# Scores from row halves, the coefficient on GpSimd, and token norms on ScalarE, in a two-layer hybrid backbone

## The chip, the cores and the metric

The kernel runs on one core of one Trainium2 chip. The metric is device time of one execution in microseconds (us). Three runs of the kernel before took 2230.95, 2233.83 and 2234.59 us, median 2233.83. A fourth execution was profiled; it took 2234.37 us, its trace spans 2232.6 us, and TensorE was granted 0.978 of its full clock on the mean.

## The reference, cut to what matters

Two layers work on 640 tokens of width 1024: 512 noisy latents (four tiles of 128) and 128 context tokens (one tile). Each layer norms and modulates the tokens, projects them, runs three mixers side by side (an RWKV-7 scan, a differential attention, a long convolution), projects their outputs together, norms, gates and adds, and then does the same around a squared-ReLU MLP. The change touches the attention and the RMS norm of the tokens:

```python
def _rmsnorm(x, g):
    xf = x.astype(jnp.float32)
    y = xf * lax.rsqrt(jnp.mean(xf * xf, axis=-1, keepdims=True) + RMS_EPS)
    return (y * g.astype(jnp.float32)).astype(x.dtype)

def _diff_attention(q, k, v, lam):
    ...
    def block(qblk):
        s = jnp.einsum('bqhmd,bkhmd->bhmqk', qblk, k).astype(jnp.float32) * scale
        p = jax.nn.softmax(s, axis=-1)
        wts = p[:, :, 0] - lam * p[:, :, 1]
        return jnp.einsum('bhqk,bkhe->bqhe', wts.astype(v.dtype), v)
    ...
```

There are four heads. A head has two maps (`m`), each with queries and keys of 64 dimensions, and values of 128. A latent query sees 640 keys (512 latents and 128 of a cache), a context query sees the 128 context keys.

## The kernel before, in words

The program is a long list of instructions for five engines: TensorE (PE), VectorE (DVE), ScalarE (ACT), GpSimd (POOL) and the DMA queues. A scheduler chooses the order on each engine when the program is built; after that each engine goes through its list in order, and an instruction that waits holds up all behind it.

One layer runs in this order: input columns of the convolution and the scan, the attention's columns, operands of the scan, attention, the scan itself (with the next modulations), the output projection with norm, and the MLP with norm. In the trace the attention of the first layer lies at 378 to 470 us and that of the second at 1443 to 1537 us. A prologue (0 to about 112 us) computes filters and modulations and norms the five token tiles.

`attention` (L609) goes over 4 heads times 5 token tiles, 20 units per layer, as a pipeline of three stages: at step n `at_scores` of unit n, `at_values` of unit n-1, `at_out` of unit n-2. At the third tile of a head, `at_head` loads the next head.

`at_head` (L636) fills two tiles of `[128, 2, 640]` floats. `kr` holds the keys with both maps stacked, map 0 in rows 0 to 63 and map 1 in rows 64 to 127: 512 latent keys after rotary embedding, the cache's 128, the context's 128. `qp` holds the queries twice, padded: plane 0 has map 0's queries in its upper rows and zeros below, plane 1 the other way round. So a matmul over all 128 rows gives the scores of one map. The zeros come from two memsets on POOL (L645, L646), the context's queries from two DMAs (L649), and the last add of the rotary embedding is done in two halves of 64 rows on DVE (L659). `at_v` (L666) takes a third tile, `vt`, for the values: five tiles of 128 tokens and the cache.

`at_scores` (L670) does for each map one matmul of 512 columns (L682) and one of 128 (L683), or for the context's unit one of 128 (L685), into the PSUM pool `pss` of two buffers; a minimum along the row on DVE (`amin`, L687) and an exponential on ACT that also gives the row's sum (`pexp`, `asum`, L689). Then the two maps are put together: DVE takes the reciprocal of the second sum (`arec`, L692), makes from it the coefficient `acf` = first sum x reciprocal x minus lambda (L694), and adds the second map times `acf` to the first (L698). POOL squares the first sum (`ae`, L696). `at_values` (L701) transposes the result on PE (`pst`), copies it (`awt`) and multiplies it with the values (`pso`, L714). `at_out` (L717) takes a sum of squares on ACT (`ass`, L723), makes the output's scale in three POOL instructions (`asm` L725, `ars` L727, `aon` L728), and transposes the scaled output on PE (`psy`).

`norm_tok` (L1422) norms one tile of 128 tokens: ACT squares it with a sum (L1426), `rstd` makes the scale on POOL, and DVE multiplies the tile by it (L1428). It is called 20 times: for the five tiles in the prologue (`xl`), and 15 times on `acc`, inside the stretches where the projections end and each layer begins.

The matmuls on the scores are on plain 32-bit floats, which PE does in two passes.

Of the kernel before, what the change touches and what calls it, by code (L numbers as in the profile page):

```python
# [12 lines left out]
AF = mybir.ActivationFunctionType  # L13
ALU = mybir.AluOpType
# [3 lines left out]
P = 128  # L18
NL = 2
TL = 512  # L20
TC = 128
T = TL + TC
NT = T // P
# [88 lines left out]
class Net:  # L112
# [524 lines left out]
    def at_head(self, l, h):  # L637

        nc, I = self.nc, self.I
        rot = [(i + 16) % 32 for i in range(32)]  # L640
        kr = self.at_tile("kr").rearrange("p a t -> p (a t)")
        nc.sync.dma_start(kr[:, TL:T], I["cache_kT"][l, h])
        nc.sync.dma_start(kr[:, T:T + TC], self.Qd[4 + h][:, TL:])
        qp = self.at_tile("qp")
        nc.gpsimd.memset(qp[64:, 0], 0.0)  # L645
        nc.gpsimd.memset(qp[:64, 1], 0.0)  # L646
        for m in range(2):
            r = slice(64 * m, 64 * m + 64)
            nc.sync.dma_start(qp[r, m, TL:], self.Qd[h][r, TL:])  # L649
        for isq in range(2):  # L650
            u, sh = (self.t(self.pS, [P, T], F32, "S", nm)[:, :TL] for nm in ("ql", "rsh"))
            nc.sync.dma_start(u, self.Qd[h if isq else 4 + h][:, :TL])
            nc.vector.stream_shuffle(sh, u, rot)
            nc.gpsimd.tensor_tensor(out=sh, in0=sh, in1=self.rope[:, 1], op=ALU.mult)
            nc.vector.tensor_tensor(out=u, in0=u, in1=self.rope[:, 0], op=ALU.mult)
            if isq:
                for m in range(2):
                    r = slice(64 * m, 64 * m + 64)
                    nc.vector.tensor_tensor(out=qp[r, m, :TL], in0=u[r], in1=sh[r], op=ALU.add)  # L659
            else:  # L660
                nc.vector.tensor_tensor(out=kr[:, :TL], in0=u, in1=sh, op=ALU.add)
        return {"kr": kr, "qp": qp}

    def at_v(self, l, h, head):
        vt = self.at_tile("vt").rearrange("p a t -> p (a t)")[:, :(NT + 1) * P].rearrange("p (j t) -> p j t", t=P)
        hs = slice(h * P, (h + 1) * P)  # L666
        self.nc.sync.dma_start(vt[:, :NT], self.Vd[:, :, hs])
        self.nc.sync.dma_start(vt[:, NT], self.I["cache_v"][l][:, hs])
        head["vt"] = vt

    def at_scores(self, u, pool):

        nc, H, j = self.nc, u["head"], u["j"]
        lat = j < 4
        nk = u["nk"] = T if lat else TC
        pm = []
        s = self.t(pool, [P, 2], F32, "asum")
        for m in range(2):
            q = H["qp"][:, m, j * P:(j + 1) * P]
            ps = self.t(self.pss, [P, 1024], F32, "pss")  # L680
            if lat:
                nc.tensor.matmul(ps[:, :TL], q, H["kr"][:, :TL], start=True, stop=True)  # L682
                nc.tensor.matmul(ps[:, TL:T], q, H["kr"][:, TL:T], start=True, stop=True)  # L683
            else:
                nc.tensor.matmul(ps[:, :TC], q, H["kr"][:, T:T + TC], start=True, stop=True)  # L685
            mn = self.t(pool, [P, 1], F32, "amin")
            nc.vector.tensor_reduce(out=mn, in_=ps[:, :nk], axis=AX.X, op=ALU.min)  # L687
            pe = self.t((self.pwh, self.pwl)[m], [P, 1024], F32, ("wh", "wl")[m], "pexp")[:, :T]
            nc.scalar.activation(pe[:, :nk], ps[:, :nk], AF.Exp, bias=mn, scale=-1.0, accum_out=s[:, m:m + 1])  # L689
            pm.append(pe)  # L690
        rc = self.t(pool, [P, 1], F32, "arec")
        nc.vector.reciprocal(rc, s[:, 1:2])  # L692
        cf = self.t(pool, [P, 1], F32, "acf")
        nc.vector.scalar_tensor_tensor(out=cf, in0=s[:, 0:1], scalar=rc, in1=self.nlam, op0=ALU.mult, op1=ALU.mult)  # L694
        e0 = u["e0"] = self.t(pool, [P, 1], F32, "ae0", bufs=4)
        nc.gpsimd.tensor_tensor(out=e0, in0=s[:, 0:1], in1=s[:, 0:1], op=ALU.mult)  # L696
        w = u["w"] = pm[0]
        nc.vector.scalar_tensor_tensor(out=w[:, :nk], in0=pm[1][:, :nk], scalar=cf, in1=w[:, :nk],  # L698
                                       op0=ALU.mult, op1=ALU.add)
# [722 lines left out]
    def norm_tok(self, x, out, pool, junk=None):  # L1422
        nc = self.nc
        ss = self.t(pool, [P, 1], F32, "ss")
        kw = {} if junk is None else {"saturate": False}
        nc.scalar.activation(out if junk is None else junk, x, AF.Square, accum_out=ss, **kw)  # L1426
        r = self.rstd(pool, ss, D, 1e-6, [P, 1])
        nc.vector.tensor_scalar(out=out, in0=x, scalar1=r, scalar2=None, op0=ALU.mult)  # L1428

    def act_tiles(self):  # L1430
        x = [self.t(self.pA, [P, 2, T], F32R, "A", f"act{k}") for k in range(KD)]
# [360 lines left out]
```

## Time and profile before

| | |
|---|---|
| runs | 2230.95, 2233.83, 2234.59 us |
| profiled execution | 2234.37 us |
| its span in the trace | 2232.6 us |
| mean granted clock of TensorE | 0.978 |
| PE busy | 94% of the span |
| DVE, ACT, POOL busy | 64%, 38%, 36% |

The difference of 1.8 us between the span and the profiled execution's time lies around the trace and is kept as it is. A share of busy time is a mean over stages with different limits, so what a stage is worth has to be read from that stage. The chain of work that ended last is followed back from the last instruction; an engine's time counts in full only where it lies on it. Matmuls overlap, so the time from one matmul's start to the next one's start says more than a matmul's own duration.

### The profile page before, as it was taken

Reading aid. Unit: us, or ns where it says so; the run is one execution under the profiler, and the core shown is the slowest. Engines: PE = TensorE matmul, PEld = TensorE weight load, DVE = VectorE, ACT = ScalarE, POOL = GpSimd, SP = SyncE. Lnnn points to the kernel's source line nnn. Section 1 sums busy time; section 2 is a strip of 40 time slices with the busy share of each in tenths; the row PEclk is TensorE's granted clock in tenths of the full one; section 3 lists DMA queues with packets and bytes.
Section 4 is the critical chain, followed back from the end, with each engine's and each line's share of the span. In section 5 each row is a group of like instructions: output and inputs, shape, how many; then the busy total and the mean of one; then the engine's idle time right before and its main releaser. Section 6 shows DMA issues by size and latency. Waiting matters only on the chain.

```text
span 2232.6 us, 34700 instructions
## 1 busy us (share of the span) xinstructions
PE 2104.0 (94%) x13620; PEld 1811.5 (81%) x13620; DVE 1425.3 (64%) x2102; ACT 849.7 (38%) x1670; POOL 806.9 (36%) x775
## 2 busy tenths in 40 slices
PE   6999998889999899999999999988999989999998
PEld 3799996667788789898988999766788788989896
DVE  6667648856675845564766674886576584637475
ACT  4542344653442623131324334465344352313131
POOL 5434434631112424251522443464112342524251
PEclk8999999999999999999999999999999999999999
DMA  8244432145405122222254243223501512222233
GB/s 306 82 153 146 137 101 80 43 146 190 154 18 197 66 82 70 88 81 78 86 179 167 97 130 101 87 67 129 188 23 56 182 44 95 80 73 93 77 104 123
DMA packets 86072, 245.46 MB, mean 110 GB/s; under 512 B 12195, under 2 KB 24995, under 8 KB 85908
## 3 DMA queue, kind: packets, MB, share of 16 engines
q1 hardware_dynamic: 80148, 222.34, 29.6%
q0 software_dynamic: 5760, 20.91, 3.0%
q8 instruction: 107, 1.75, 0.3%
q14 instruction: 57, 0.47, 0.1%
HBM read 214.80 MB, written 28.87 MB: 109 GB/s over the span
## 4 chain that ended last, share of the span: by engine, by line
PE 37%; DVE 8%; issue 5%; DMA 4%; POOL 4%; ACT 2%; SPq 0%; POOLq 0%; DVEq 0%; ACTq 0%
PE psA L388 5%; PE psB L176 5%; PE psB L177 5%; PE psB L175 5%; PE psF L177 2%; PE psF L176 2%; PE psF L175 2%; DMA ffb<-in_w_ff_dram 1%; DMA wr<-in_w_mod_dram 1%; PE b L1023 1%; POOL fft L457 1%; DVE wl L143 1%; DVE ffr L497 1%; PE pss L682 1%; PE psD L175 1%
## 5 line engine op out<-in xcount | busy, mean ns | idle before, releaser
L388 PE MATMUL psA<-act,wh 128*128 128x320 f32 x1472 | 300.4, 317 | 0.9 <-ACT uhr L1513 0.5
L388 PEld LDWEIGHTS psA<-act,wh 128*128 128x128 f32 x1472 | 236.9, 191 | 9.5 <-issue 6.8
L177 PE MATMUL psB<-wh,f 128*128 128x512 f32 x560 | 218.1, 389 | 0.0
L176 PE MATMUL psB<-wl,f 128*128 128x512 f32 x560 | 218.0, 389 | 0.0
L143 POOL TENSOR_TENSOR wl<-wr,wh 128x1024 fp32r<-128x1024 f32 x42 | 103.8, 2472 | 305.1 <-ACT wh L147 150.6
L175 PE MATMUL psB<-wh,f 128*128 128x512 f32 x560 | 209.1, 389 | 0.0
L388 PE MATMUL psA<-act,wl 128*128 128x320 f32 x736 | 179.5, 316 | 2.4 <-DVE wl L143 2.4
L143 DVE TENSOR_TENSOR wl<-wr,wh 128x1024 fp32r<-128x1024 f32 x84 | 109.7, 1306 | 83.0 <-ACT wh L147 74.6
L147 ACT CAST wh<-wr 128x1024 fp32r<-128x1024 f32 x75 | 78.7, 1049 | 188.3 <-PE psB L177 87.7
L457 POOL TENSOR_TENSOR fft<-ffb 128x512 f32<-128x512 f32 x56 | 92.1, 1644 | 129.7 <-DVE wl L143 56.2
L388 PEld LDWEIGHTS psA<-act,wl 128*128 128x128 f32 x736 | 126.4, 191 | 5.2 <-DVE wl L143 3.4
L177 PEld LDWEIGHTS psB<-wh,f 128*128 128x128 f32 x560 | 105.1, 188 | 22.0
L175 PEld LDWEIGHTS psB<-wh,f 128*128 128x128 f32 x560 | 105.1, 188 | 21.6
L176 PEld LDWEIGHTS psB<-wl,f 128*128 128x128 f32 x560 | 105.1, 188 | 21.6
L147 ACT CAST f<-ffr 128x640 fp32r<-128x640 f32 x64 | 43.7, 726 | 154.2 <-DVE ffr L497 154.2
L1052 DVE TENSOR_TENSOR x<-b,cmask 128x512 f16<-128x512 f32 x120 | 80.3, 685 | 31.8 <-PE b L1051 31.3
L1061 ACT CAST t<-px 128x512 f16<-128x512 f32 x100 | 58.5, 588 | 103.8 <-PE px L1056 103.0
L149 DVE CAST wh<-wr 128x1024 fp32r<-128x1024 f32 x51 | 41.8, 819 | 84.1 <-PE psB L177 63.9
L505 DVE TENSOR_TENSOR ffr<-ffr,psF 128x320 f32<-128x320 f32 x140 | 67.3, 481 | 36.5 <-POOL ffr L505 20.3
L505 POOL TENSOR_TENSOR ffr<-ffr 128x320 f32<-128x320 f32 x56 | 54.2, 967 | 92.6 <-DVE ffr L505 87.6
L1023 PE MATMUL b<-ZR,bp 128*128 128x256 f32 x320 | 85.6, 392 | 0.8 <-ACT awt L147 0.7
L176 PE MATMUL psF<-ffS,sh 128*128 128x320 f32 x256 | 80.0, 313 | 5.8 <-DVE ffS L143 5.8
(463 smaller groups left out, 6000.9 us busy)
## 6 DMA issues: line engine op xcount, KB each, us to landing
wr<-in_w_mod_dram SPq DMA_DIRECT2D x83, 512.0 KB
wr<-in_w_ff_dram SPq DMA_DIRECT2D x72, 512.0 KB
wr<-in_w_in_dram SPq DMA_DIRECT2D x46, 512.0 KB
x<-x SPq DMA_DIRECT2D x30, 512.0 KB
ffa<-in_w_ff_dram SPq DMA_DIRECT2D x28, 512.0 KB
ffb<-in_w_ff_dram SPq DMA_DIRECT2D x28, 512.0 KB
dft<-in_k_dftf_dram POOLq DMA_DIRECT2D x16, 512.0 KB, 7.6
dft<-in_k_dfti_dram POOLq DMA_DIRECT2D x16, 512.0 KB, 5.0
```

The lines of the kernel that those rows point to most:

```text
L143: eng.tensor_tensor(out=l, in0=src, in1=h.bitcast(F32), op=ALU.subtract)
L147: self.nc.scalar.copy(out, in_)
L149: self.nc.vector.tensor_copy(out, in_)
L175: nc.tensor.matmul(out, a[0], b[0], start=first, stop=False)
L176: nc.tensor.matmul(out, a[0], b[1], start=False, stop=False)
L177: nc.tensor.matmul(out, a[1], b[0], start=False, stop=last)
L388: self.nc.tensor.matmul(ps[:, hf, :320], (h, l)[a][:, k * P:(k + 1) * P], act[b][k][:, hf * 320:hf * 320 + 320], start=k == 0 and i == 0, ...
L457: sub = lambda o, x, y: nc.gpsimd.tensor_tensor(out=o, in0=x, in1=y, op=ALU.subtract)
L505: add = lambda o, a, b, e=nc.vector, op=ALU.add: e.tensor_tensor(out=o, in0=a, in1=b, op=op)
L1023: nc.tensor.matmul(ps[:, 2 * e:2 * e + 2], bp[:, q, e], s["ZR"][:, :, j], start=True, stop=True)
L1052: nc.vector.tensor_tensor(out=vw(x16), in0=vw(ps), in1=cm(i), op=ALU.mult)
L1061: nc.scalar.copy(t16, ps1)
```

## The change

Four things change.

1. The queries are no longer padded. `at_head` writes all 128 rows of the rotated queries by one add into `vq`, and a map's scores are taken by matmuls over the 64 rows `r` of that map alone, in queries and keys. The memsets of zeros go, and the two DMAs of context queries become one, into the free columns 768 to 895 of `kr`.
2. A head has two tiles instead of three: the values take columns 0 to 767 of `vq` and the latent queries columns 768 to 1279. `vq` is taken in `at_head` and filled with values by `at_v` as before.
3. The coefficient `acf` is made by a `tensor_scalar` of two per-row scalars on POOL instead of DVE's `scalar_tensor_tensor`.
4. In `norm_tok` the multiplication by the scale is an activation `Copy` with a per-row scale on ACT instead of a DVE `tensor_scalar`.

```diff
--- before.py
+++ after.py
@@ -638,31 +638,24 @@
 
         nc, I = self.nc, self.I
         rot = [(i + 16) % 32 for i in range(32)]
+
         kr = self.at_tile("kr").rearrange("p a t -> p (a t)")
+        vq = self.at_tile("vq").rearrange("p a t -> p (a t)")
         nc.sync.dma_start(kr[:, TL:T], I["cache_kT"][l, h])
         nc.sync.dma_start(kr[:, T:T + TC], self.Qd[4 + h][:, TL:])
-        qp = self.at_tile("qp")
-        nc.gpsimd.memset(qp[64:, 0], 0.0)
-        nc.gpsimd.memset(qp[:64, 1], 0.0)
-        for m in range(2):
-            r = slice(64 * m, 64 * m + 64)
-            nc.sync.dma_start(qp[r, m, TL:], self.Qd[h][r, TL:])
+        nc.sync.dma_start(kr[:, T + TC:T + 2 * TC], self.Qd[h][:, TL:])
+        q = vq[:, 768:]
         for isq in range(2):
             u, sh = (self.t(self.pS, [P, T], F32, "S", nm)[:, :TL] for nm in ("ql", "rsh"))
             nc.sync.dma_start(u, self.Qd[h if isq else 4 + h][:, :TL])
             nc.vector.stream_shuffle(sh, u, rot)
             nc.gpsimd.tensor_tensor(out=sh, in0=sh, in1=self.rope[:, 1], op=ALU.mult)
             nc.vector.tensor_tensor(out=u, in0=u, in1=self.rope[:, 0], op=ALU.mult)
-            if isq:
-                for m in range(2):
-                    r = slice(64 * m, 64 * m + 64)
-                    nc.vector.tensor_tensor(out=qp[r, m, :TL], in0=u[r], in1=sh[r], op=ALU.add)
-            else:
-                nc.vector.tensor_tensor(out=kr[:, :TL], in0=u, in1=sh, op=ALU.add)
-        return {"kr": kr, "qp": qp}
+            nc.vector.tensor_tensor(out=q if isq else kr[:, :TL], in0=u, in1=sh, op=ALU.add)
+        return {"kr": kr, "vq": vq}
 
     def at_v(self, l, h, head):
-        vt = self.at_tile("vt").rearrange("p a t -> p (a t)")[:, :(NT + 1) * P].rearrange("p (j t) -> p j t", t=P)
+        vt = head["vq"][:, :(NT + 1) * P].rearrange("p (j t) -> p j t", t=P)
         hs = slice(h * P, (h + 1) * P)
         self.nc.sync.dma_start(vt[:, :NT], self.Vd[:, :, hs])
         self.nc.sync.dma_start(vt[:, NT], self.I["cache_v"][l][:, hs])
@@ -676,13 +669,12 @@
         pm = []
         s = self.t(pool, [P, 2], F32, "asum")
         for m in range(2):
-            q = H["qp"][:, m, j * P:(j + 1) * P]
+
+            r = slice(64 * m, 64 * m + 64)
+            q = H["vq"][r, 768 + j * P:768 + (j + 1) * P] if lat else H["kr"][r, T + TC:T + 2 * TC]
             ps = self.t(self.pss, [P, 1024], F32, "pss")
-            if lat:
-                nc.tensor.matmul(ps[:, :TL], q, H["kr"][:, :TL], start=True, stop=True)
-                nc.tensor.matmul(ps[:, TL:T], q, H["kr"][:, TL:T], start=True, stop=True)
-            else:
-                nc.tensor.matmul(ps[:, :TC], q, H["kr"][:, T:T + TC], start=True, stop=True)
+            for a, b, o in ((0, TL, 0), (TL, T, TL)) if lat else ((T, T + TC, 0),):
+                nc.tensor.matmul(ps[:, o:o + b - a], q, H["kr"][r, a:b], start=True, stop=True)
             mn = self.t(pool, [P, 1], F32, "amin")
             nc.vector.tensor_reduce(out=mn, in_=ps[:, :nk], axis=AX.X, op=ALU.min)
             pe = self.t((self.pwh, self.pwl)[m], [P, 1024], F32, ("wh", "wl")[m], "pexp")[:, :T]
@@ -691,7 +683,7 @@
         rc = self.t(pool, [P, 1], F32, "arec")
         nc.vector.reciprocal(rc, s[:, 1:2])
         cf = self.t(pool, [P, 1], F32, "acf")
-        nc.vector.scalar_tensor_tensor(out=cf, in0=s[:, 0:1], scalar=rc, in1=self.nlam, op0=ALU.mult, op1=ALU.mult)
+        nc.gpsimd.tensor_scalar(out=cf, in0=s[:, 0:1], scalar1=rc, scalar2=self.nlam, op0=ALU.mult, op1=ALU.mult)
         e0 = u["e0"] = self.t(pool, [P, 1], F32, "ae0", bufs=4)
         nc.gpsimd.tensor_tensor(out=e0, in0=s[:, 0:1], in1=s[:, 0:1], op=ALU.mult)
         w = u["w"] = pm[0]
@@ -1425,7 +1417,7 @@
         kw = {} if junk is None else {"saturate": False}
         nc.scalar.activation(out if junk is None else junk, x, AF.Square, accum_out=ss, **kw)
         r = self.rstd(pool, ss, D, 1e-6, [P, 1])
-        nc.vector.tensor_scalar(out=out, in0=x, scalar1=r, scalar2=None, op0=ALU.mult)
+        nc.scalar.activation(out, x, AF.Copy, scale=r)
 
     def act_tiles(self):
         x = [self.t(self.pA, [P, 2, T], F32R, "A", f"act{k}") for k in range(KD)]
```

The lines behind `at_head` move up by 8 in the changed kernel (L682 is L677, L694 is L686).

The scheduler sets the orders anew. On PE, in the first layer's attention (scores of the third head, products with the second's values), this stands before. `pss` are scores, `psy` and `pst` transposes, `pso` products with the values:

```order
L682 MATMUL pss_4234<-kr_4014,qp_4017 128x512
L683 MATMUL pss_4234<-kr_4014,qp_4017 128x128
L170 MATMUL psy_4185<-ident_134,aon_4177 128x128
L682 MATMUL pss_4241<-kr_4014,qp_4017 128x512
L683 MATMUL pss_4241<-kr_4014,qp_4017 128x128
L714 MATMUL pso_4218<-vt_3917,awt_4214 128x128
L170 MATMUL pst_4256<-ident_134,pexp_4198 128x128 x4
L170 MATMUL pst_4262<-ident_134,pexp_4198 128x128
```

And in the changed kernel:

```order
L677 MATMUL pss_4219<-kr_4004,vq_4005 128x512
L677 MATMUL pss_4219<-kr_4004,vq_4005 128x128
L170 MATMUL psy_4171<-ident_134,aon_4163 128x128
L677 MATMUL pss_4226<-kr_4004,vq_4005 128x512
L677 MATMUL pss_4226<-kr_4004,vq_4005 128x128
L706 MATMUL pso_4203<-vq_3739,awt_4199 128x128
L170 MATMUL pst_4241<-ident_134,pexp_4183 128x128 x4
L170 MATMUL pst_4247<-ident_134,pexp_4183 128x128
```

Here the sequence is the same: the scores of two maps, which now fill 64 rows, with full-height matmuls between them and on both sides. Where score matmuls follow each other with nothing between them I call that a stretch. By the orders there are 35 stretches in a layer before and after; in the changed kernel 8 of the 70 hold both maps of a latent unit, as rows that follow each other.

On POOL, at the load of the last head in the first layer, before (`ae` the squared sum, `qp` the padded queries, `asm`, `ars`, `aon` the scale of an output; `mbias` belongs to a later stage):

```order
L696 TENSOR_TENSOR ae_911_4107<-asum_4088 128x1
L645 MEMSET qp_4288 64x640
L646 MEMSET qp_4288 64x640
L725 TENSOR_SCALAR asm_4131<-ae_865_3981,ass_4129 128x1
L696 TENSOR_TENSOR ae_931_4156<-asum_4139 128x1
L270 MEMSET mbias_5389 128x512
L727 TENSOR_TENSOR ars_4133<-asm_4131,mhalf_87 128x1
L725 TENSOR_SCALAR asm_4180<-ae_891_4056,ass_4178 128x1
L728 TENSOR_SCALAR aon_4128<-ao_4075,ars_4133 128x128
```

And in the changed kernel, on POOL, two units on:

```order
L688 TENSOR_TENSOR ae_969_4237<-asum_4218 128x1
L717 TENSOR_SCALAR asm_4261<-ae_929_4142,ass_4259 128x1
L719 TENSOR_TENSOR ars_4263<-asm_4261,mhalf_87 128x1
L720 TENSOR_SCALAR aon_4258<-ao_4205,ars_4263 128x128
L686 TENSOR_SCALAR acf_4235<-asum_4218,arec_4233,nlam_549 128x1
L688 TENSOR_TENSOR ae_995_4308<-asum_4289 128x1
```

The memsets are gone, and `acf` of a unit (its `asum` ends in 4218) stands behind the three scale instructions of the unit two before, not in front of them. It stands so in 11 of the 20 units of the first layer.

On DVE, before:

```order
L692 RECIPROCAL arec_4207<-asum_4192 128x1
L694 SCALAR_TENSOR_TENSOR acf_4209<-asum_4192,arec_4207,nlam_549 128x1
L698 SCALAR_TENSOR_TENSOR pexp_4198<-pexp_4205,acf_4209,pexp_4198 128x640
L687 TENSOR_REDUCE amin_4237<-pss_4234 128x1
L687 TENSOR_REDUCE amin_4244<-pss_4241 128x1
```

And in the changed kernel, at the unit with `asum_4177`:

```order
L684 RECIPROCAL arec_4192<-asum_4177 128x1
L690 SCALAR_TENSOR_TENSOR pexp_4183<-pexp_4190,acf_4194,pexp_4183 128x640
L679 TENSOR_REDUCE amin_4222<-pss_4219 128x1
L679 TENSOR_REDUCE amin_4229<-pss_4226 128x1
L149 COPY awt_4240<-pst_4241 128x512
```

The coefficient is gone from between the reciprocal and the sum of the two maps, which waits for POOL there; the minima of the next unit's maps (`amin`) are queued behind it.

## Rows read from the trace of the kernel before

**Rows 1.** Busy us (instructions) by stretch: start:end, length, PE, PEld, DVE, ACT, POOL, clock, DMA.

```profile
12.00:90.00 78.00, 62.62 (x334) 40.36 (x335) 57.04 (x98) 42.77 (x82) 39.93 (x39) 0.82 0.64 232
378.00:470.00 92.00, 81.02 (x447) 58.47 (x447) 74.05 (x144) 57.85 (x191) 50.09 (x90) 0.98 0.19 59
1443.00:1537.00 94.00, 83.25 (x459) 59.85 (x458) 74.27 (x144) 60.19 (x195) 50.74 (x91) 0.98 0.20 63
```

**Rows 2.** Chain that ended last, 1443 to 1537 us: start, us, what.

```profile
1444.62 0.79 PE pss L682 x2
...
1453.63 3.65 DMA ql<-qk
...
1524.61 1.11 PE pss L682 x2
```

**Rows 3.** Timeline of PE, attention: start, us, operation, shapes, count.

```profile
413.77 1.02 PE L682 MATMUL pss<-kr,qp 128*128 128x512 f32 x2
414.63 0.38 PE L683 MATMUL pss<-kr,qp 128*128 128x128 f32 x2
414.85 0.27 PE L170 MATMUL psy<-ident,aon 128*128 128x128 f32 x1
```

**Rows 4.** Timeline of PE around four matmuls of 64 rows.

```profile
303.02 0.75 PE L388 MATMUL psA<-act,wh 128*128 128x320 f32 x4
303.61 0.46 PE L388 MATMUL psA<-act,wl 128*128 128x320 f32 x2
303.90 0.38 PE L170 MATMUL pshb<-ident,ksq 128*128 128x128 f32 x2
304.21 1.34 PE L585 MATMUL ps<-u,w 64*128 64x320 f32 x4
305.48 0.85 PE L388 MATMUL psA<-act,wh 128*128 128x320 f32 x4
306.17 0.46 PE L388 MATMUL psA<-act,wl 128*128 128x320 f32 x2
```

**Rows 5.** Groups by line and shape, 378 to 470 us: count, busy us, mean ns, idle.

```profile
L694 DVE SCALAR_TENSOR_TENSOR acf<-asum,arec,nlam 128x1 f32<-128x1 f32 x20 | 6.4, 319 | 0.3
```

**Rows 6.** Timeline of DVE and POOL in one unit.

```profile
432.33 0.26 POOL L725 TENSOR_SCALAR asm<-ae,ass 128x1 f32<-128x1 f32 x1
...
433.35 0.61 POOL L728 TENSOR_SCALAR aon<-ao,ars 128x128 f32<-128x128 f32 x1
...
434.18 0.15 DVE L692 RECIPROCAL arec<-asum 128x1 f32<-128x1 f32 x1
...
434.37 0.22 DVE L694 SCALAR_TENSOR_TENSOR acf<-asum,arec,nlam 128x1 f32<-128x1 f32 x1
434.62 0.89 DVE L698 SCALAR_TENSOR_TENSOR pexp<-pexp,acf,pexp 128x640 f32<-128x640 f32 x1
```

**Rows 7.** Chain at a hand-over from DVE (L1416) to POOL (L374).

```profile
1155.48 0.08 issue
1155.56 0.20 POOL prsm L374
```

**Rows 8.** Instructions on the tile qp: count, least/median/most ns, first to last.

```profile
L659 DVE TENSOR_TENSOR qp<-ql,rsh x16: 673/687/6149, 353.3 to 1489.6; 64x512 f32<-64x512 f32 x16
L645 POOL MEMSET qp<- x8: 626/626/630, 352.2 to 1488.1; 64x640 f32 x8
L649 SPq DMA_DIRECT2D qp<-qk x16: 450/530/603, 352.3 to 1489.4; - x16
```

**Rows 9.** The token norm's lines, in the same columns.

```profile
L1428 DVE TENSOR_SCALAR acc<-x,rstd x15: 746/751/1780, 720.0 to 1796.2; 128x1024 f32<-128x1024 f32 x15
L1428 DVE TENSOR_SCALAR xl<-xl,rstd x5: 734/754/1749, 24.1 to 46.0; 128x1024 f32<-128x1024 f32 x5
L1426 ACT ACTIVATE acc<-x x15: 1047/1061/1065, 717.6 to 1793.7; 128x1024 f32<-128x1024 f32 x15
```

**Rows 10.** One group of the page: matmuls of 32 columns of weights.

```profile
L292 PE MATMUL psmod<-wr,sc 128*32 128x256 f32 x664 | 57.0, 388 | 9.6 <-DMA wr<-in_w_mod_dram 9.2
```

## The prediction

> **What bounds the kernel now.** I read the busy time by stretch first. In the first layer's attention PE is busy 81.0 of 92 us, DVE 74.1, ACT 57.9 and POOL 50.1; the second layer's is alike [rows 1]. So PE leads but has 11 us free, and DVE is next with 18: neither engine alone sets the time, units of work pass from PE to DVE to ACT to DVE to PE, and whichever is late at a hand-over counts. In the prologue the clock is 0.82, PE is busy 62.6 of 78 us and DVE 57.0 [rows 1].
>
> Then the chain of waits, to see how often the work that the change touches sets the end. In the second layer's attention it runs through 18 stretches of score matmuls, 16 on 640 keys, of which the first and the last stand in [rows 2], and two of context units. The orders have 35 such stretches in a layer, so a delay at a stretch counts about half the time. The chain also holds the transfer of a head's raw queries or keys, 3.65 us [rows 2]: a head's load is not hidden everywhere. In the timeline of PE a map's scores take, start to start, 2 x 0.43 us for 512 columns in two passes and 2 x 0.11 us for 128, with nothing lost on either side [rows 3].
>
> **The change part by part.** The scores from row halves do not shorten a matmul: its columns set its time, and they stay. What is new is that PE goes from 128 rows to 64 and back around each stretch. The trace has one other place where 128-wide weights fill 64 rows, four matmuls of 320 columns between full ones [rows 4]. Two transposes ahead of them take 0.31 us from start to start, where two passes of 128 columns take 0.22 [rows 3]: 0.09 for going in. The four take 1.27 us (304.21 to 305.48); 320 columns at the rate of [rows 3] are 0.43 x 320/512 = 0.27, four 1.08: 0.19 for the first weights and going out. The next group of four takes 0.69 us (305.48 to 306.17) and its like before 0.59 (303.02 to 303.61): 0.10 for the weights behind. That is 0.38 us a trip. With 70 stretches it is 26.6 us of PE in both layers; 18 of 35 lie on the path, so I take +14. Bounds: if PE's free 11 us a layer swallow all they can, 26.6 - 22 = +5; if all of it is late, +27.
>
> The Trainium skill (page "TensorEngine Tiling (Array Packing)", section "Key Properties") says that a change of the tiling mode drains TensorE, while a change of the tile alone does not. Rows 4 agree with the first half, 0.38 us for going to 64 rows and back; no row here shows the second. By the rule I count a stretch once though its maps use different rows; if each of the 80 maps paid, it would be 10 more trips, 3.8 us, half on the path: +2.
>
> The coefficient on POOL takes one instruction from DVE, 20 times 0.32 us in the mean or 6.4 us a layer [rows 5], and puts two hand-overs in its place. Between the reciprocal's end (434.18 + 0.15 = 434.33) and the sum of the maps (434.62) lay 0.29 us [rows 6]. Now it is a hand-over to POOL, 0.08 [rows 7], a small `tensor_scalar` there, 0.26 as for `asm` [rows 6], and a hand-over back, taken as 0.08 too: 0.42, so +0.13 a unit, 5.2 us for 40 units, half on the path: +2.6. POOL is also busy 50.1 of 92 us, so at 54% of the arrivals something runs there; half of 0.61 us (`aon` [rows 6]) is 0.3, times 0.54 times 40 is 6.5 us, half on the path +3. I take +5 for both. Behind the sum that waits stand the next minima on DVE, and behind these the exponentials and the PSUM buffers that PE needs, which is why I don't hide it. Bounds: if DVE's relief counts and the hand-overs fall into waits, half of 12.8 us, -6. If in 11 of 20 units the coefficient waits out half of the three instructions in front of it (432.33 to 433.96, 1.63 us [rows 6]), 22 x 0.8 = 18, half on the path, 9 + 2.6 = +12.
>
> The load of a head loses a second add of queries (0.69 us), two memsets (0.63 each) and one DMA (0.53) [rows 8]; over 8 heads 5.5 + 10 + 4.2 = 20 us, one bound if every one were waited for; the other is 0, if the loads have slack. In layer 0 the first head's load lies ahead of the first scores, and POOL's memsets stand there in front of its rotary products; -2. In layer 1 I take the add, -0.7. For the six later heads, loaded three units ahead of use, I take the DMA that stood in front of the raw queries in SP's queue, since their transfer is on the chain [rows 2]: 6 x 0.53 = -3. Together -6, near the middle of the bounds. One of the sixteen adds took 6.15 us [rows 8], a wait while POOL worked; I don't count it as saved, since the rotary products that held it stay. Two tiles a head instead of three I cost at nothing: eight buffers held the tiles of two heads and two thirds before and no wait for them is on the chain.
>
> The norms on ScalarE: DVE took 0.75 us a tile when alone and up to 1.78 when something held it; ACT takes 1.06 for the squares of the same size [rows 9], which I take for the `Copy`. So +0.3 where DVE was free and -0.7 where not. At the 15 places between stages these about cancel where they lie on the path, 0. In the prologue five tiles leave DVE, the engine busier than ACT by 14 us [rows 1], 3.8 us by their median, and most of that is PE's wait: -3. Bounds: 20 x 0.3 = +6 if ACT's square of the next tile queues behind every copy; -8 if DVE's 15 us in all come back by half.
>
> The sum: 14 + 5 - 6 - 3 = +10 us. On the profiled execution's 2234.4 us, 0.5 us from the median of the runs, that gives 2244 us.
>
> **The rivals.** First, faster: PE's slack takes the trips, +5, DVE's relief counts, -6, loads and norms give -8 and -3. That is -12, 2222 us. For it speaks that PE waits 11 us a layer and that DVE loses 6.4 us of coefficients and 5.5 us of adds [rows 1, 5, 8]. Against it: the score stretches are on the chain, 18 of 35, so PE is not the one with slack there [rows 2].
>
> Second, the parts balance within 4 us: trips +8, coefficient +2, loads -6, norms -3, or 2235 us. It needs a trip cheaper than at [rows 4], for example because a stretch of only two matmuls leaves less to refill.
>
> Third, the two row halves work side by side. In the trace 664 matmuls on 32 columns of weights are busy 57.0 us together though one lasts 388 ns in the mean [rows 10], so some run at once. A second map then costs nothing where both stand together, in 8 of 70 stretches: 8 x 1.08, half on the path, -4, and if the halves also cost no trips, 10 - 14 - 4 = -8, 2226 us. Against it stand the orders, where something full-height nearly always separates the maps, and the 0.38 us of [rows 4]. The Trainium skill (page "TensorE: Matmul & The Clock Gate", section "Part 3: Packing small matmuls — row/col tiling") says that matmuls on different groups of rows run concurrently; only rows of column groups show that here.
>
> Fourth, much slower: the coefficient is stuck on POOL. In 11 of 20 units it is queued behind three instructions that wait for an ACT sum of squares. If that sum ends later than the reciprocal by 0.4 us or more, DVE stands still with the next minima behind it, and a unit loses about 1.2 us (the rest of the sum and most of the 1.63 us [rows 6]): 22 x 1.2 = 26 instead of 5, so 2244 + 21 = 2265 us. Against it: in [rows 6] the three began 1.85 us ahead of the reciprocal.
>
> **How the numbers follow.** The forecast, slower by about 10 us, gets 0.50; within it the trips decide between 2236 and 2252, its own range. Faster by slack 0.25, balanced 0.08, side by side 0.05, stuck on POOL 0.12. The low ends add up to 5 - 6 - 20 - 8 = -29 and the high ones to 27 + 12 + 0 + 6 = +45; that all fall on one side is unlikely, and I leave a tenth below 2226 and a tenth above 2259. About 0.2%, 4.5 us, is what a measurement of this kernel can tell from no change, so 2229.4 to 2238.3 is the same. Faster: most of the first and the third, 0.21 + 0.04, and 0.01: 0.26. Same: the balanced case and the edges of the forecast and the first, 0.08 + 0.08 + 0.04 = 0.20. Slower: the rest, 0.54.
>
> **What would show it.** In the profile after: the matmuls of 64 rows have a longer group time than 0.86 + 0.22 us, start to start, by about 0.3, and the full-height ones behind them too; PE's busy time in the attentions rises by some 10 us each. The coefficient on POOL starts within 0.3 us of the reciprocal's end, and DVE's wait ahead of the sum of the maps has POOL as releaser. The stretch of an attention is longer by 5 to 8 us, the prologue shorter by about 3. It is wrong if score groups keep 1.08 us and no gap opens beside them; if attentions shorten, the slack of PE was real and the first rival holds.

## The result, and the profile after

The changed kernel takes 2250.8 us (median of 5 runs, 2247.2 to 2262.4), the kernel before in the same comparison 2234.5: a ratio of 1.0089, 95% interval 1.0071 to 1.0107. It is slower, as forecast, but by 16 us by the medians and 20 by the ratio, and not by 10. The profiled execution took 2247.2 us with a span of 2245.5 us, and TensorE's mean granted clock fell from 0.978 to 0.973; over the five runs it is 0.963 to 0.973. The clock is a term that the forecast's sum does not have. One run of a later kernel, 2275.64 us of the layout with row halves alone, counts as slow and is left out of its median, ratio, clock and line.

Busy time by stretch of the kernel after, in the columns of [rows 1], with one more stretch:

```profile
12.00:90.00 78.00, 62.26 (x354) 40.28 (x355) 53.65 (x94) 49.04 (x87) 38.57 (x39) 0.85 0.65 232
378.00:470.00 92.00, 85.50 (x377) 56.45 (x375) 58.30 (x104) 51.32 (x166) 46.74 (x92) 0.85 0.15 45
1443.00:1537.00 94.00, 85.81 (x417) 58.33 (x416) 62.77 (x113) 52.69 (x168) 48.91 (x91) 0.93 0.18 58
396.50:426.50 30.00, 28.90 (x83) 18.22 (x82) 15.08 (x28) 10.99 (x37) 11.81 (x23) 0.54 0.09 28
```

In the first attention PE is busier than before (85.5 against 81.0 us in the same 92) yet does fewer matmuls (377 against 447), at a clock of 0.85 instead of 0.98. The last row says where: for 30 us TensorE runs at 0.54, nearly its half level, 1.2 GHz of 2.4, while it is busy 28.9 of the 30 us. DVE, ACT and POOL are busy less than before; a part of the attention's work now lies behind 470 us, since its last transpose `psy` starts at 489.1 us and before at 479.1.

From the first score matmul to the last transpose `psy` the attentions took 100.5 and 100.9 us before and take 114.6 and 107.4 now: +20.6. All the rest of the span became 7.8 us shorter. Windows of 4 us of the kernel before, around the same place of the first attention (columns as above; the clock is third from the end):

```profile
396.00:400.00 4.00, 2.30 (x20) 2.02 (x18) 3.21 (x8) 2.27 (x9) 2.85 (x5) 1.00 0.00 0
400.00:404.00 4.00, 3.50 (x11) 2.37 (x11) 3.96 (x7) 1.01 (x6) 3.61 (x6) 0.59 0.31 86
404.00:408.00 4.00, 4.00 (x28) 3.28 (x27) 3.19 (x10) 2.65 (x10) 2.20 (x5) 0.98 0.30 95
```

And of the kernel after:

```profile
396.00:400.00 4.00, 3.15 (x12) 1.33 (x10) 4.00 (x12) 1.94 (x8) 3.70 (x7) 0.81 0.31 87
400.00:404.00 4.00, 4.00 (x15) 3.12 (x15) 3.71 (x5) 0.78 (x4) 2.71 (x3) 0.50 0.11 30
404.00:408.00 4.00, 3.75 (x11) 2.09 (x11) 1.08 (x2) 1.25 (x5) 1.73 (x4) 0.50 0.01 2
...
420.00:424.00 4.00, 4.00 (x11) 2.50 (x11) 2.44 (x3) 1.25 (x3) 1.20 (x3) 0.50 0.00 0
424.00:428.00 4.00, 4.00 (x18) 3.05 (x17) 0.67 (x2) 2.23 (x8) 1.02 (x3) 0.77 0.01 4
```

Both kernels fall to the half level here, after PE had waited: 2.30 us busy of 4 before, 3.15 after. Before, the clock is back by the next row of the table, with PE busy on 128 rows. After, PE is just as busy and the clock stays down from 400 to 424 us. What PE does differently there is that every other group of matmuls in its timeline has 64 rows. At the half level a map's scores take 2.43 us instead of 1.28, as the timeline of PE shows:

```profile
403.77 2.50 PE L677 MATMUL pss<-kr,vq 64*128 64x512 f32 x4
406.20 1.33 PE L170 MATMUL pst<-ident,pexp 128*128 128x128 f32 x5
```

At the full clock the timeline answers [rows 3] so:

```profile
443.03 1.38 PE L706 MATMUL pso<-vq,awt 128*128 128x128 f32 x10
444.34 1.34 PE L677 MATMUL pss<-kr,vq 64*128 64x512 f32 x4
445.62 0.33 PE L170 MATMUL psy<-ident,aon 128*128 128x128 f32 x1
445.87 1.34 PE L677 MATMUL pss<-kr,vq 64*128 64x512 f32 x4
447.15 0.77 PE L170 MATMUL pst<-ident,pexp 128*128 128x128 f32 x5
...
1503.27 1.36 PE L677 MATMUL pss<-kr,vq 64*128 64x512 f32 x8
1504.55 0.76 PE L170 MATMUL pst<-ident,pexp 128*128 128x128 f32 x5
```

A map takes 1.28 us from start to start (444.34 to 445.62) where it took 1.08, and the single transpose behind it 0.25 where it took 0.11. The ten `pso` ahead take 1.31 for 10 x 0.11. So a trip to 64 rows and back costs 0.20 + 0.14, or 0.20 + 0.21, about the 0.38 us that was forecast. At 1503.27 both maps of a unit stand together: their eight passes take 1.28 us, the same as four of one map. The two row halves do run side by side, as the third rival had it, in the seven places of this trace where they meet.

The chain of the second attention, answering [rows 2], holds score pieces of twice the length where the clock is low:

```profile
1457.23 2.42 PE pss L677 x4
...
1460.91 2.43 PE pss L677 x4
```

The coefficient on POOL (its line: least, median, most ns; then who waited, us, times):

```profile
L686 POOL TENSOR_SCALAR acf<-asum,arec,nlam x40: 334/340/1292, 381.3 to 1548.8; 128x1 f32<-128x1 f32 x40
...
  DVE pexp L690: 13.0, 26
```

It costs 0.34 us, not 0.26, and DVE waits for it 13 us in both layers together. The norm's product on ACT takes 1.15 us instead of the 1.06 assumed:

```profile
L1420 ACT ACTIVATE acc<-x,rstd x15: 1136/1150/1157, 727.1 to 1807.1; 128x1024 f32<-128x1024 f32 x15
L1420 ACT ACTIVATE xl<-xl,rstd x5: 1145/1147/1149, 24.5 to 46.0; 128x1024 f32<-128x1024 f32 x5
```

### The profile page after: what moved, and what is told of

Its sections match the earlier page's. It is cut to its first block, busy times and chain, and to the rows that moved or that the text cites. A ratio compares the mean times of both kernels' runs of the same rounds, so it can differ in the third digit from the quotient of the medians.

```text
span 2245.5 us, 34682 instructions
## 1 busy us (share of the span) xinstructions
PE 2123.2 (95%) x13620; PEld 1817.3 (81%) x13620; DVE 1391.8 (62%) x2034; ACT 872.1 (39%) x1690; POOL 806.6 (36%) x799
## 4 chain that ended last, share of the span: by engine, by line
PE 46%; DVE 5%; POOL 3%; issue 2%; DMA 2%; ACT 2%; SPq 0%; POOLq 0%; DVEq 0%; ACTq 0%
PE psB L176 5%; PE psB L177 5%; PE psB L175 5%; PE psA L388 5%; PE psF L177 3%; PE psF L175 3%; PE psF L176 3%; PE pss L677 1%; PE b L1015 1%; PE psD L175 1%; PE psD L177 1%; PE psD L176 1%; DMA wr<-in_w_mod_dram 1%; PE pso L706 1%; DMA ffb<-in_w_ff_dram 1%
## 5 line engine op out<-in xcount | busy, mean ns | idle before, releaser
L677 PE MATMUL pss<-kr,vq 64*128 64x512 f32 (+1 forms) x256 | 87.8, 508 | 9.9 <-DVE vs L149 5.6
```

Of the source, the lines that this page charges most:

```text
L677: nc.tensor.matmul(ps[:, o:o + b - a], q, H["kr"][r, a:b], start=True, stop=True)
```

## The experiments

Each kernel was timed against the kernel before on the same chip; medians and ratios are of those comparisons, and the clock is the mean over a kernel's runs. Kernels told as "the layout" are the changed kernel with parts put back.

**The layout with row halves alone.** The coefficient goes back to DVE, the norm's product too.

```diff
-        nc.gpsimd.tensor_scalar(out=cf, in0=s[:, 0:1], scalar1=rc, scalar2=self.nlam, op0=ALU.mult, op1=ALU.mult)
+        nc.vector.scalar_tensor_tensor(out=cf, in0=s[:, 0:1], scalar=rc, in1=self.nlam, op0=ALU.mult, op1=ALU.mult)
-        nc.scalar.activation(out, x, AF.Copy, scale=r)
+        nc.vector.tensor_scalar(out=out, in0=x, scalar1=r, scalar2=None, op0=ALU.mult)
```

> The change's layout alone: two tiles a head and scores from 64 rows; the coefficient and the norm's product stay on DVE. In the profile of the changed kernel TensorE's granted clock is at half level for some 24 us in a row in the first layer's attention (397 to 426 us), before for 3. Theory clock: the half-height matmuls lengthen the time at half level, and each such us costs up to half a us of path. Then this kernel has a lower mean clock than before (0.965 to 0.973 against 0.978), varies by several us between runs, and is slower by 12 to 25 us. Theory trips: the clock's drop comes from something else (the waits on POOL or ACT) and only 0.4 us a trip is paid here, 70 times, half to all on the path, less 6 us for the loads: slower by 8 to 21 us at an unchanged clock of 0.978. Theory POOL: the coefficient carries the loss; then this one is within 6 us of before.

Measured: 2250.5 us against 2231.3, ratio 1.0096 (1.0065 to 1.0128), clock 0.972. Theory POOL falls. The five runs scatter over 25 us, and time and clock go together: 2238.8 us at 0.977, 2250.5 at 0.974, 2250.2 at 0.973, 2256.6 at 0.970, 2264.2 at 0.966. A line through them has a slope of 2190 us per unit of clock and meets 0.980, the mean clock of before in this comparison, at 2235 us: 4 us over before's mean of 2230.7. The other 17 of the 21 us between the means go with the clock.

**The rest without the row halves:** before, with only the two edits that the last diff takes back.

> The other half: padded queries over all 128 rows in three tiles as before, but the coefficient on POOL and the norm's product on ACT. Theory clock and theory trips: without half-height matmuls the clock is as before (0.978) and the time is 2229 to 2237 us. Theory POOL: 2243 us or more, with DVE waiting for POOL ahead of the sum of the maps.

Measured: 2224.7 us, ratio 0.9975 (0.9963 to 0.9988), clock 0.981. Only this kernel and that of the norm below are faster than before with an interval clear of 1, and it says that the whole loss is in the row halves and their layout.

**Only the coefficient on POOL.**

> Only the coefficient on POOL. The prediction's term is +5 us (bounds -6 and +12). Theory POOL: +10 us or more. Theories clock and trips: within 5 us of before, at its clock.

Measured: 2229.3 us, ratio 0.9993 (0.9981 to 1.0004). Theory POOL falls a second time. DVE waits here 17.5 us for POOL in 26 places, in 18 of the 40 units `aon` stands directly ahead of the coefficient on POOL, and still the attentions are shorter by 5.3 us in the profiled execution (97.9 and 98.2).

**Only the norm's product on ACT.**

> Only the norm's product on ACT. The prediction's term is -3 us (bounds -8 and +6): faster by 3 in the prologue and in the norms between stages, no change in the attentions.

Measured: 2225.9 us, ratio 0.9980 (0.9967 to 0.9993). The size is near the forecast's -3, and so is most of the place. Busy time of the prologue and of a stretch behind it, of the kernel before and, below, of this one:

```profile
0.00:112.00 112.00, 89.07 (x498) 61.53 (x499) 75.20 (x132) 53.80 (x99) 55.51 (x56) 0.88 0.55 193
200.00:216.00 16.00, 13.04 (x73) 12.25 (x72) 14.90 (x17) 4.72 (x8) 10.14 (x7) 0.79 0.22 67
```

```profile
0.00:112.00 112.00, 88.96 (x517) 61.76 (x517) 73.56 (x131) 59.77 (x104) 54.41 (x56) 0.89 0.56 198
200.00:216.00 16.00, 15.89 (x107) 15.55 (x107) 15.41 (x18) 6.98 (x11) 9.73 (x9) 0.90 0.16 54
```

In the prologue this kernel gets 19 matmuls further, some 2.8 us by the 600 that the kernel before does in the next 88 us; by 250 us it is 29 ahead (1446 against 1417), some 4.3 us. The difference is won at 200 us, where PE of both kernels waits and falls to the lower level and here is back sooner; the scheduler's new order has a part in that, which was not separated.

**Trips without half-height work.** Into the kernel before:

```diff
             ps = self.t(self.pss, [P, 1024], F32, "pss")
+            nc.tensor.matmul(ps[:, :32], q[:64], H["kr"][:64, :32], start=True, stop=True)
             if lat:
```

> The kernel before with one small matmul of 64 rows and 32 columns ahead of each map's scores, into the same buffer, where the scores overwrite it: 80 trips to 64 rows and back, while all the scores still run over 128 rows. Theory columns (half-height streaming lowers the clock): the clock stays at 0.978 to 0.982 and only the trips are paid, 80 x 0.4 = 32 us of TensorE, on the path between a third and all: +8 to +30 us, and the runs differ as little as before's. Theory pauses (the breaks at each trip lower the clock): the clock falls to 0.961 to 0.977 as with the row halves, the runs scatter over some 30 us.

Measured: 2250.2 us against 2234.1, ratio 1.0071 (1.0056 to 1.0085), and a clock of 0.980, in six runs within 6 us. Theory pauses falls: 80 trips, each with its breaks, leave the clock where it was. In the timeline a trip reads:

```profile
424.90 0.71 PE L170 MATMUL pst<-ident,pexp 128*128 128x128 f32 x5
425.54 0.41 PE L681 MATMUL pss<-kr,qp 64*128 64x32 f32 x2
425.87 1.13 PE L683 MATMUL pss<-kr,qp 128*128 128x512 f32 x2
426.83 0.38 PE L684 MATMUL pss<-kr,qp 128*128 128x128 f32 x2
```

The transposes take 0.64 us for five times 0.11, the two short matmuls 0.33, the long ones 0.96 for 0.86: 0.09 + 0.33 + 0.10 = 0.52, of which 2 x 0.03 us are the 32 columns at the rate of [rows 3]. So 0.46 a trip, 37 us of TensorE for 80; 16 us of it reach the end, 43%. In proportion the trips of 70 stretches would be 14 us, the forecast's first term. The window that was at the half level, here at full clock, of this kernel and of the layout with row halves:

```profile
398.00:422.00 24.00, 23.60 (x130) 17.05 (x129) 18.97 (x40) 14.79 (x52) 15.61 (x27) 1.00 0.19 61
```

```profile
398.00:422.00 24.00, 23.44 (x66) 15.34 (x66) 13.29 (x24) 8.78 (x30) 8.97 (x17) 0.50 0.09 26
```

PE is as busy in the one as in the other.

**The row halves alone,** in the kernel before with its padded queries, three tiles and loads:

```diff
+            r = slice(64 * m, 64 * m + 64)
+            q = q[r]
...
-                nc.tensor.matmul(ps[:, :TL], q, H["kr"][:, :TL], start=True, stop=True)
+                nc.tensor.matmul(ps[:, :TL], q, H["kr"][r, :TL], start=True, stop=True)
```

> The smallest edit: the kernel before with its padded queries, three tiles and loads, only that both maps' scores are taken from their 64 rows of them. If the row halves alone carry the loss, it is as the layout with them: clock near 0.970, about +20 us, runs scattered over some 30 us. If the two tiles or the loads had a part in the clock's fall, the clock stays nearer 0.98 and it is +9 to +16 us, the trips alone.

Measured: 2260.5 us against 2227.9, ratio 1.0150 (1.0124 to 1.0176), clock 0.968. This one line carries more than the whole loss. In its trace the instructions of every engine follow each other as in the kernel before, one for one, so no new order has a part in it. By the line through its runs (2253.0 us at 0.973 to 2272.9 at 0.963) it would be at 2240 us with a clock of 0.980, 12 us over before, which would be the trips. That is read beyond the clocks it had.

**One map of two.** `r = slice(0, 64) if m == 0 else slice(0, P)` in the same place.

> The kernel before, with map 0 alone taken from 64 rows (the queries stay padded, nothing else changes); map 1 over 128 rows. 40 trips, half the columns at half height. Theory columns: clock between before's 0.980 and the row halves' 0.971, time between, about +10 us. Theory threshold-like: nearly nothing at the clock, and 40 x 0.4 = 16 us of TensorE, half on the path, +8 us.

Measured: 2237.1 us against 2234.1, ratio 1.0019 (1.0007 to 1.0032), clock 0.979, in the order of the kernel before. The clock does not fall, as the second theory said; the time is below both theories: 40 trips cost 3 to 4 us, far less than half of the 16 that 80 of them cost.

**Three units of five.** `r = slice(64 * m, 64 * m + 64) if j < 3 else slice(0, P)`.

> The same for three units of five (the first three latent tiles of each head); the fourth and the context's over all rows: 48 trips, three quarters of the long score matmuls. The run with one map in halves (40 trips, half of the columns) kept its clock at 0.979 and lost 4 us. If the clock's time at half level grows with the share of half-height columns in the row, this is between: 0.974 to 0.977 and +8 to +15 us. If it needs both maps of a unit in halves to stay low, it is as with all, 0.970 to 0.974 and +13 to +20.

Measured: 2244.5 us against 2227.9, ratio 1.0073 (1.0056 to 1.0090), clock 0.974, again in the order of before. It lies between one map and all, but it does not decide between the two readings: the clock is the edge of both ranges, the time, +16, is just in that of the second only, and by a share of the columns the run of one map should have lost clock too. Where its profile is at the lower level, and where that of all halves is:

```profile
1452.00:1476.00 24.00, 21.68 (x61) 12.86 (x59) 13.96 (x29) 9.48 (x26) 8.61 (x13) 0.57 0.25 79
```

```profile
1464.00:1500.00 36.00, 34.41 (x130) 23.15 (x129) 24.56 (x47) 17.10 (x57) 18.69 (x30) 0.70 0.13 41
```

The low stretches lie in different places in the two profiles; PE is busy nine tenths of the time in them.

**The layout without row halves:** `r = slice(0, P)` in the layout run. Both maps then have the same scores, the sum of the two.

> The layout alone without half-height matmuls: two tiles a head, unpadded queries, one add, one DMA, no memsets, but scores over all 128 rows (so each map's scores are the sum of both maps'; coefficient and norm on DVE as before). It shows what the load of a head gives by itself. The prediction's term is -6 us (bounds 0 and -20): 2225 us at before's clock of 0.98. From the row halves' runs at that clock, 2235 us by the line through them, less the trips at 0.2 us each of 67, 2221 us.

Measured: 2231.2 us against 2230.2, ratio 1.0003 (0.9993 to 1.0014), clock 0.979. The loads give nothing by themselves. In the trace every engine has the same order as in the layout with row halves, 2250.5 us and 0.972, so the height of the scores alone makes that difference.

**Full-height filler.** In the layout with row halves:

```diff
+            nc.tensor.matmul(ps[:, :256], self.ident, H["kr"][:, T:T + 256], start=True, stop=True)
             for a, b, o in ((0, TL, 0), (TL, T, TL)) if lat else ((T, T + TC, 0),):
```

> The layout with row halves as in the run of it alone, and ahead of each map's scores one full-height matmul of 256 columns into the same buffer, overwritten by the scores: 80 x 0.22 = 17 us more of TensorE. Theory clock by half-height columns: the added full-height work brings the granted clock back up from 0.971 towards 0.98, so the time falls by up to 20 us for that and rises by about 9 for the work on the path: at or below 2253 us, and the runs scatter less. Theory breaks: the clock stays near 0.971 and the time rises by 9 us or more, to 2262.

Measured: 2282.0 us, ratio 1.0236 (1.0216 to 1.0256), clock 0.975. The clock rose by less than half of the way from 0.972 to 0.98, but the time rose by some 30 us, more than either theory gave. The first 24 us of its first attention are at the half level in spite of the filler, with PE busy throughout:

```profile
374.00:398.00 24.00, 23.93 (x52) 13.22 (x53) 8.32 (x16) 7.14 (x18) 1.49 (x4) 0.51 0.38 119
398.00:505.00 107.00, 103.57 (x562) 69.07 (x562) 68.34 (x133) 57.50 (x188) 49.21 (x89) 1.00 0.12 40
```

The filler stands in front of every score and undoes the places where two maps ran side by side, so its time tells nothing on the clock; the rise of the clock speaks at most weakly for the first theory.

**Both maps side by side,** and its control over 128 rows. One PSUM tile for both maps, single-buffered:

```diff
-            self.psum(ca, pss=2, pst=1, pso=1)
+            self.psum(ca, pss=1, pst=1, pso=1)
...
+        pss = self.t(self.pss, [P, 2, 1024], F32, "pss")
+        pss = [pss[:, m] for m in range(2)]
+        for a, b, o in ((0, TL, 0), (TL, T, TL)) if lat else ((T, T + TC, 0),):
+            for m in range(2):
...
+                nc.tensor.matmul(pss[m][:, o:o + b - a], q, H["kr"][r, a:b], start=True, stop=True)
```

> The changed kernel with both maps' scores of a unit side by side: one PSUM tile for both maps, single-buffered, the four matmuls in the order map 0, map 1, map 0, map 1. In the profile of the changed kernel the one place where both maps stood together took 1.28 us for two maps, and one map alone took 1.28 too. So 32 latent units save 1.1 us of TensorE and one trip of 0.4 each, some 48 us in both layers, and half of it was on the path: -24 against the changed kernel. The single buffer costs what the next unit's scores wait for the exponentials. If the clock follows from half the array being idle it stays near 0.98, and the time is 2215 to 2235 us; if 64-row matmuls as such lower it, 0.97 and 2235 to 2250.

> The control to the paired maps: the same single PSUM tile for both maps and the same order, but padded queries over 128 rows (coefficient on POOL and norm on ACT as in the changed kernel). What this is slower than the same kernel with two buffers (2224.7 us) is the price of the single buffer: 0 to +20 us. The difference to the paired row halves is what running side by side gives: about 32 x 0.9 us less the trips of 0.4 in 40 units, 12 us or so on TensorE.

Measured: 2292.5 us, ratio 1.0254 (1.0234 to 1.0275), and for the control 2312.0, ratio 1.0349 (1.0333 to 1.0366). My price for the single buffer was wrong by far: some 84 us, +78 where the same kernel with two buffers (2224.7) was -6. PE waits for the exponentials ahead of each unit, here in the paired kernel:

```profile
428.92 1.35 PE L677 MATMUL pss<-kr,vq 64*128 64x512 f32 x8 [1.02 <-ACT pexp L683]
430.58 0.74 PE L170 MATMUL pst<-ident,pexp 128*128 128x128 f32 x5 [0.31 <-DVE pexp L692]
```

The pairing itself holds: eight passes in 1.35 us, and 19.5 us less than the control. Two such tiles at once, twice the PSUM that the scores had, were not tried, so the pairing without the wait stays open.

On the clock the two say something else. Its mean is 0.958 in the paired kernel and 0.969 in the control. The stretch of the first attention, of the paired kernel and then of the control:

```profile
378.00:500.00 122.00, 88.25 (x450) 62.09 (x451) 68.29 (x120) 59.77 (x193) 57.52 (x107) 0.80 0.13 41
378.00:500.00 122.00, 88.89 (x397) 60.20 (x396) 61.80 (x108) 53.20 (x168) 49.73 (x98) 0.86 0.12 39
```

The control has only full-height scores, and with PE idle 33 of 122 us its clock is low too: row halves are not the only way to a lower clock. With the same single buffer the row halves lie another 0.010 below, though the loads and the orders of the two differ as well. The bounds expected for the paired kernel, 0.98 or 0.97, did not count on the waits, so it does not decide between its two readings.

## Why the prediction was right in direction and wrong in size

**The step that failed** is the first term: "The scores from row halves do not shorten a matmul: its columns set its time, and they stay." They stay at one clock. The sum priced the trips and let the clock be what it was. The runs put two things in place of the one: the trips (80 of them 16 us, at an unchanged clock; 12 us by the line of the row halves alone), and the clock, which was left out at no price. It falls from 0.980 to 0.968 where row halves are the only change, and 21 of 33 us go with it by the line through those runs; in the layout it is 17 of 21 us. An estimate from the profiled executions points the same way: if TensorE sets the pace throughout, the clock's lost share times the span is 0.022 x 2232.6 = 49 us before and 0.027 x 2245.5 = 61 us after, 12 us more, and the span grew by 12.9. The trips' own term was sized rightly, 0.38 us each forecast and 0.34 to 0.46 found, 43% of 80 trips on the path against 18 of 35 assumed. The fall of the clock came with the row halves and not with the breaks: trips alone left it at 0.980, one map of each unit in halves at 0.979, three units of five 0.974, all 0.968 to 0.972, and the layout at full height at 0.979.

**The coefficient on POOL** was forecast at +5 and is -2 by its median (interval of the ratio 0.9981 to 1.0004). The hand-over is even dearer than assumed, 0.34 us on POOL, and DVE does wait. What was left out of the chosen value, and is likely what pays for this, is the relief that I kept only as a bound: 20 times 0.32 us of DVE less in each attention [rows 5], in a stretch where DVE is nearly as loaded as PE. The rival with the coefficient stuck on POOL is refuted.

**The loads** were forecast at -6 and give 0 when alone (ratio 1.0003, 0.9993 to 1.0014), although DMA, memsets and add are gone. That six of the eight heads are loaded far enough ahead is the likely reason, but was not tested. With row halves the layout is better than the bare halves, 2250.5 us against 2260.5, and by their two lines at a clock of 0.98 still by some 7 us, 4 over before against 11 to 12; why it helps there and not at full height stays open.

**The norm** was forecast at -3 and is -4 to -5: some 2.8 us of it in the prologue, as forecast, and about 1.5 from PE's shorter stop at 200 us, which the forecast did not have.

**The sum.** 14 - 2 + 0 - 5 = +7 without the clock, where the forecast's was +10. That these are close is in part luck: the coefficient was 7 too high and the loads 6 too low, and the two cancel. The changed kernel's own five runs, by a line of 1500 us per unit of clock, meet 0.980 at 2236 us, 2 over before's mean of 2234, and the other 16 go with the clock; the line is read beyond the clocks it had. So the parts, each measured in a kernel of its own, add up to some 5 us too much. Which one is too high was not found; the trips may be, since 40 of them cost only 3 to 4 us. In the profiled executions the first attention grew by 14.1 us and the second by 6.5, where 5 to 8 each were forecast, and the rest of the span shrank by 7.8.

**Rivals.** The third's mechanism exists, eight passes in 1.28 us, but only where two maps meet, as the orders had it; its time was wrong because nothing forms such pairs elsewhere. Those rows agree with the Trainium skill's rule on concurrent row groups (page "TensorE: Matmul & The Clock Gate", section "Part 3: Packing small matmuls — row/col tiling"). The first rival's time is refuted, its loads above all; PE's slack is not. By its rule the 37 us of the 80 trips would cost 37 - 22 = 15, by the half that I took 19, and 16 was measured; that 40 trips cost 3 to 4 us speaks for slack as well. Even without the clock's fall the change would have been no faster, +2 to +7.

**What stays open.** That the clock falls with the row halves is shown, by kernels that differ from their controls in the rows alone and have the same orders. How much it falls with how many of them is not: one map of two cost no clock, three units of five half of the fall. Nor is it shown why it falls at a given moment: the falls shown here at about 400 us began after PE had waited, the control of the paired maps has a low clock without any row halves, and the filler's run did not isolate what keeps the clock down under a busy PE. How the loss divides into trips and clock rests on lines that reach beyond their runs.

## What to carry to other kernels

Before changing how many rows of TensorE a matmul fills, price three things: the trips between heights (about 0.4 us each here), the matmuls at the clock that the stretch will be granted, and whether two halves really stand side by side in the order. A stretch that already falls to the lower clock after a wait, and recovers, is a place where such a change may not recover. And when the granted clock differs between two profiles, plot the runs' times against their clocks before explaining anything by waits.

## What was unexpected of the hardware

Padded queries fill 128 rows with as many zeros as data, and the kernel's clock is 0.98; the same products from 64 rows, in the same order, bring it to 0.968. TensorE was busy 28.9 of 30 us at a clock of 0.54. And two 64-row halves on different rows took 1.28 us together, as long as one alone.
